# First mixer's input projection: a pipeline in program order with sums held in PSUM, and a last group that alternates convolution and attention blocks

## The chip, the cores and the metric

The kernel runs on one core of one Trainium2 chip. The metric is device time in microseconds (us) of one execution. TensorE (PE) multiplies matrices into PSUM, VectorE (DVE) and ScalarE (ACT) work on tiles elementwise, GpSimd (POOL) builds masks, and SyncE (SP) issues the DMAs that bring data from device memory. PEld is the weight load of TensorE, which overlaps with its matmuls.

## What is computed

Two layers on one sequence of 256 positions with 2048 features, all in float32. Each layer normalises x, scales and shifts it by a modulation (a matrix-vector product with the activated vector `c`), mixes along the sequence, and adds an MLP. The change touches the modulation, the norm and the mixer of layer 0, cut here to its frame:

```python
c_act = jax.nn.silu(c)
mod = jnp.einsum('bd,de->be', c_act, mod_w[layer]) + mod_b[layer]
sh1, sc1, g1, sh2, sc2, g2 = [m[:, None, :] for m in jnp.split(mod, 6, axis=-1)]
h = rms_norm(x, norm_mix_w[layer]) * (1.0 + sc1) + sh1
proj = jnp.einsum('btd,de->bte', h, w_in)
gq, gk, gv, gz, gb, ga, aq, ak, av = split_sizes(proj, AB_SPLITS)
o_a = gated_deltanet(gq, gk, gv, gz, gb, ga, conv_w, a_log, dt_bias, norm_w)
o_b = chunk_band_attention(aq, ak, av, q_norm_w, k_norm_w, rel_bias)
mix = jnp.einsum('bte,ed->btd', jnp.concatenate([o_a, o_b], axis=-1), w_out)
x = x + g1 * mix
```

`gated_deltanet` runs a causal convolution of width 4 over its q, k and v, normalises q and k, and solves a triangular system for each chunk of positions; `chunk_band_attention` normalises q and k and attends over the sequence with a bias. Each has eight heads of width 128, worked on in two groups of four.

## The kernel before

Activations lie with features on partitions. A **unit** is a block of 512 normalised features: four tiles of 128 features by 256 positions. The input projection is cut into **items**: one item multiplies one unit (a "row group" `kg`, 0 to 3) by one block of 512 output columns, with one 1 MB weight block (`w[kg, c0]`, a tile of 128 x 2048, two halves of 1024). The blocks are named by their columns: `GQ`, `GK`, `GV` for the delta net's q, k, v (two blocks each, the second `GQ + 1` and so on), `AQ`, `AK`, `AV` for attention, `GZ` for the gate. A convolution-type item (`b_item`, line 501) has the weights as the stationary operand and matmuls 256 wide; an attention-type item (`a_item`, line 527) has the activations stationary and matmuls 512 wide.

A product in float32 is made in one of two ways. **Split**: weights and activations are each cut into a high part of reduced precision and a remainder. ACT casts the weights to `wh` (line 317), DVE subtracts to get `wl` (line 321), and PE adds three products, `wh` by high, `wh` by remainder, `wl` by high. **Whole**: one plain float32 matmul (two records in the trace) on the loaded weights, with neither cast nor subtraction; it needs an unsplit copy of the unit, `hw`. Before, only the last unit has `hw` (`norm_unit` with `whole`, line 849).

The modulation is 192 sums on DVE (line 439, `mod_job`): each takes a 1 MB matrix `mraw` (128 x 2048), multiplies it by the row vector `crow` and adds along the row, which gives one column of 128 values. Additions of the bias and the scale's gain (lines 447 and 449) finish two columns at a time. The unit of row group `kg` needs shift (`v` = 0) and scale (`v` = 1) for four columns.

The program is written out as one stream. `emit` loads and splits an item's weights one item ahead of its matmuls. After each piece of an item `tick` advances a list of short tasks (`fast`: evacuations, norms), a list of background work (`bg`: the chunk solve, the attention scores) and, by `rate`, the generator of modulation sums. A scheduler then fixes the order on each engine; instructions passed to `keep_in_program_order` stay where they are written. SP's queue issues the loads in order, each waiting for its buffer: four `raw` buffers for weights and modulation matrices together, four pairs of `wh` and `wl`, 18 unit buffers `u`.

In `run` (line 1536) the start loads x, takes square sums (ten narrow matmuls with `ones`, lines 809 to 834) and makes eight modulation sums for unit 0 before the first weights. Row groups 0 to 2 (the **head**) then run the same eight items, `GK, GQ, GV, GK + 1, GQ + 1, GV + 1, AQ, AK`. The first two keep their sums over the groups in PSUM buffers `pm`; the other six go through `pg`, of which there are two: each item's result is copied (line 1590) or added on DVE (line 1592) to a partial sum in a unit buffer. The last group runs the eight items with row group 3, with the remaining attention and gate blocks (all four row groups each) between them, while the chunk solve runs in the background: transposes of `gX`, products `gX` by `gLt`, a masked copy `gY` (DVE, line 1108), products `gXt` by `gY`, and a subtraction from `gX` (DVE, line 1114). Then the output projection starts (`pw`).

## Time and profile before

| | us |
|---|---|
| runs of the kernel before | 2718.03 (median), 2714.11, 2718.79 |
| the profiled execution, own time | 2719.37 |
| its span, first to last instruction | 2717.6 |
| mean granted TensorE clock | 0.998 |
| first weight matmul starts | 40.16 |
| row groups 0 to 2 end | 185.79 |
| output projection starts | 491.30 |

The page gives each engine's busy time and share of the span; the windows view the same for stretches of it. The chain that ended last is followed back from the last instruction, each step to what released it. A timeline row has start, length, engine, line, operation, output<-input, shapes and count; in brackets the idle time before it and the releaser. Groups of instructions have a count, then busy time and mean ns of one.

### The profile page before, as it was taken

To read this page: it belongs to the slowest core of one execution; us is meant where nothing else is said; L and a number is where in the kernel's file an instruction comes from. 1 tells how busy PE (TensorE), PEld (TensorE's weight loads), DVE (VectorE), ACT (ScalarE), POOL (GpSimd) and SP (SyncE) were. 2 spreads that over 40 slices of the span, in tenths; PEclk is the share of its full clock that TensorE was granted. 3 is DMA by queue.
4 is the path that set the end of the run, shared out by engine and by line. 5 is a ranking of instruction groups with operands and counts; after the bars stand their busy time and mean duration, and the time that the engine had idled before them with its cause. 6 is when DMAs were issued, how large, how long until landed. Compare 5 with 4: busy or idle time off the path is not lost.

```text
span 2717.6 us, 39677 instructions
## 1 busy us (share of the span) xinstructions
PE 2665.0 (98%) x15664; PEld 2350.4 (86%) x15664; DVE 2147.6 (79%) x3081; ACT 1351.2 (50%) x1976; POOL 24.5 (1%) x98
## 2 busy tenths in 40 slices
PE   5999999999999999999999999999999999999999
PEld 5887989888888888888888888888888888888888
DVE  7998998987888888889889876897777855555554
ACT  3444454546445354454556544665555354454452
POOL 1000000000000000000000000000000000000000
PEclk9999999999999999999999999999999999999999
DMA  9986487867899898988456665554558855555554
GB/s 341 353 325 235 172 301 272 294 241 282 322 339 328 328 336 330 333 331 307 165 185 217 217 234 200 203 185 172 196 177 293 324 201 188 188 191 193 186 192 134
DMA packets 100459, 680.06 MB, mean 250 GB/s; under 512 B 11185, under 2 KB 14513, under 8 KB 19377
## 3 DMA queue, kind: packets, MB, share of 16 engines
q1 hardware_dynamic: 95376, 669.07, 68.5%
q10 hardware_dynamic: 4896, 8.46, 1.0%
q8 instruction: 123, 2.02, 0.3%
q14 instruction: 64, 0.52, 0.1%
HBM read 675.33 MB, written 2.16 MB: 249 GB/s over the span
## 4 chain that ended last, share of the span: by engine, by line
PE 90%; DVE 6%; DMA 1%; ACT 1%; issue 1%; SPq 0%; ACTq 0%; DVEq 0%
PE pw L308 70%; PE pg L308 13%; PE pm L311 4%; PE pm L308 3%; DVE mraw L439 2%; DVE wl L321 1%; PE pm L314 1%; DMA mraw<-in_mod_dram 1%; DVE u L1592 0%; ACT wh L317 0%; DVE hf L862 0%; ACT pm L1042 0%; DMA raw<-in_w_ab_dram 0%; DMA x<-in_x_dram 0%; DVE u L865 0%
## 5 line engine op out<-in xcount | busy, mean ns | idle before, releaser
L317 ACT CAST wh<-raw 128x1024 fp32r<-128x1024 f32 x870 | 907.1, 1051 | 1031.6 <-PE pw L308 732.9
L321 DVE TENSOR_TENSOR wl<-raw,wh 128x1024 fp32r<-128x1024 f32 x870 | 1048.7, 1220 | 463.8 <-ACT wh L317 349.6
L308 PE MATMUL pw<-u,wh 128*128 128x512 f32 x5584 | 1321.6, 391 | 2.6 <-DVE pad L973 1.9
L308 PEld LDWEIGHTS pw<-u,wh 128*128 128x128 f32 x5584 | 1032.2, 188 | 208.2 <-issue 3.3
L308 PEld LDWEIGHTS pw<-u,wl 128*128 128x128 f32 x5584 | 702.3, 191 | 21.3 <-issue 2.1
L308 PE MATMUL pw<-u,wl 128*128 128x256 f32 x5584 | 714.5, 283 | 0.3 <-DVE wl L321 0.3
L439 DVE SCALAR_TENSOR_TENSOR mraw<-mraw,crow 128x2048 f32<-128x2048 f32 x192 | 438.0, 2283 | 17.8 <-DMA mraw<-in_mod_dram 17.5
L308 PE MATMUL pg<-wh,u 128*128 128x512 f32 x864 | 281.6, 397 | 0.0
L308 PEld LDWEIGHTS pg<-wh,u 128*128 128x128 f32 x864 | 161.9, 188 | 32.1 <-issue 0.5
L925 DVE SCALAR_TENSOR_TENSOR x<-pw,mod,x 128x256 f32<-128x256 f32 x352 | 161.1, 478 | 22.6 <-PE pw L308 20.3
L308 PE MATMUL pg<-wl,u 128*128 128x512 f32 x432 | 169.9, 393 | 0.7 <-DVE wl L321 0.5
L308 PE MATMUL pg<-u,wh 128*128 128x256 f32 x672 | 124.6, 285 | 0.0
L308 PEld LDWEIGHTS pg<-u,wh 128*128 128x128 f32 x672 | 105.7, 192 | 0.3
L308 PEld LDWEIGHTS pg<-wl,u 128*128 128x128 f32 x432 | 81.4, 188 | 17.6 <-DVE wl L321 2.1
L308 PE MATMUL pg<-u,wl 128*128 128x256 f32 x336 | 95.3, 284 | 0.0
L308 PE MATMUL pm<-u,wh 128*128 128x256 f32 (+1 forms) x304 | 64.6, 310 | 19.2 <-ACT wh L317 19.2
L308 PEld LDWEIGHTS pm<-u,wh 128*128 128x128 f32 x304 | 49.1, 198 | 20.3 <-ACT wh L317 20.0
L308 PEld LDWEIGHTS pg<-u,wl 128*128 128x128 f32 x336 | 64.4, 192 | 0.1
L984 DVE SCALAR_TENSOR_TENSOR u<-pad,cst,u 128x256 f32<-128x256 f32 x144 | 60.6, 477 | 3.3 <-ACT u L978 3.2
L864 ACT ACTIVATE u<-hf,mod 128x256 fp32r<-128x256 f32 x64 | 29.3, 502 | 53.0 <-DVE hf L862 53.0
L1504 ACT ACTIVATE rl<-rs 128x512 f32<-128x512 f32 x64 | 40.4, 632 | 18.9 <-DVE rs L1499 14.4
L308 PE MATMUL pm<-u,wl 128*128 128x256 f32 x176 | 46.1, 290 | 3.1 <-DVE wl L321 3.1
(299 smaller groups left out, 1580.5 us busy)
## 6 DMA issues: line engine op xcount, KB each, us to landing
raw<-in_w_dram SPq DMA_DIRECT2D x256, 1024.0 KB, 5.0
mraw<-in_mod_dram SPq DMA_DIRECT2D x192, 1024.0 KB, 6.0
raw<-in_w_ab_dram SPq DMA_DIRECT2D x56, 1024.0 KB, 5.7
raw<-in_w_ssd_dram SPq DMA_DIRECT2D x48, 1024.0 KB, 4.9
raw<-in_w_sz_dram SPq DMA_DIRECT2D x32, 1024.0 KB, 4.9
raw<-in_wo_ssd_dram SPq DMA_DIRECT2D x32, 1024.0 KB, 4.8
raw<-in_wo_ab_dram SPq DMA_DIRECT2D x16, 1024.0 KB, 5.2
sE<-sd_rowd ACTq DMA_DIRECT2D x32, 256.0 KB, 4.9
```

The costliest lines, as they stand in the source:

```text
L308: self.nc.tensor.matmul(o, a, b, start=start, stop=stop, skip_group_check=True)
L311: self.nc.tensor.matmul(o, lhsT, rhs, start=True, stop=True, skip_group_check=True)
L314: self.nc.tensor.transpose(o, a, self.ident[:k, :k])
L317: a = self.nc.scalar.copy(hi, src)
L321: b = self.nc.vector.tensor_tensor(lo, src, hi.bitcast(F32), op=ALU.subtract)
L439: x = nc.vector.scalar_tensor_tensor(raw, raw, 1.0, self.crow, op0=ALU.mult, op1=ALU.mult, accum_out=t[:, f : f + 1])
L864: nc.scalar.activation(hi, h[:, f], AF.Identity, bias=shift[:, col])
L925: nc.vector.scalar_tensor_tensor(x[:, 2 * b + f], ps[:, f, n], g[:, 2 * cb + f : 2 * cb + f + 1], x[:, 2 * b + f], op0=ALU.mult, op1=ALU.add)
L984: nc.vector.scalar_tensor_tensor(h, pad[:, f, 1 + q : 257 + q], w[:, q, j : j + 1], h, op0=ALU.mult, op1=ALU.add)
L1504: nc.scalar.activation(rl, lo, AF.Relu)
```

## The change

**Start.** The loads stand in the order that the code gives. Square sums are accumulated on DVE (seven additions 512 wide) and need four narrow matmuls. One scale column is computed on PE: its matrix is packed as `mod0` for the stationary side, and 16 plain float32 matmuls one column wide give it (`mod_pe`). The norm's transposes stand behind them. `norm_first` multiplies x by the row factors `R` (DVE), scales and shifts on ACT, and keeps the unsplit unit for every row group. The first half unit needs two modulation columns only.

**Head.** `in_order` keeps all its instructions in program order, and `in_units` loads weights as two 512 KB halves into unit buffers (19 now), so that `raw` buffers hold modulation matrices only. Four first halves come first (`k0` whole, `q0` split, `v0` whole, `k1` split), then the second halves and the rest of row group 0, then groups 1 and 2. An item's matmuls over two or three row groups follow each other where listed, with the sum kept in PSUM and evacuated once, by ACT copies. The 24 items are 14 of convolution and 10 of attention type (18 and 6 before); three attention items, one convolution item and two convolution halves are whole (none before). Modulation sums have fixed places: 32 stand ahead of the head's end (31 before).

**Last group.** 18 convolution and 14 attention items (14 and 18 before), six and one of them whole (three and two before), alternating, with the last additions made in the conversion (`att_v`, `conv` write into the partial tile). `rate` goes from 0 to 0.25, 0.6, 1.1 and 0.5. `conv`'s second part has a priority of 100.

```diff
-        self.u_p = pool("up", 18)
+        self.u_p = pool("up", 19)
...
+    def mod_pe(self, raw, o):
+        for k in range(16):
+            self.mmx(o, raw[:, k * P : k * P + P], self.cact[:, k : k + 1], k == 0, k == 15)
...
+            if units:
+                raw = [self.unit(shape=[P, 1024]) for _ in hfs]
+                for hf, r in zip(hfs, raw):
+                    self.dma(r, src[:, 1024 * hf : 1024 * hf + 1024])
...
+    def norm_first(self, cb, key, acts, now=False):
...
+        for b in range(2):
+            self.ordered(nc.vector.tensor_tensor(x[b], self.x[cb][:, 2 * b : 2 * b + 2], self.row(self.R, 2), op=ALU.mult))
+            if now and b == 0:
+                yield
+        yield
+        for b in range(2):
+            for f in range(2):
+                col = slice(cb * 4 + 2 * b + f, cb * 4 + 2 * b + f + 1)
+                self.ordered(nc.scalar.activation(x[b][:, f], x[b][:, f], AF.Identity, scale=scale[:, col], bias=shift[:, col]))
+            self.split(x[b], p[b][:, :, 0], p[b][:, :, 1])
...
+        chunk("k0", 0, True, (0,))
+        raws = [self.mod_load(mod[0, 0, 2])]
+        chunk("q0", 0, False, (0,))
+        raws.append(self.mod_load(mod[0, 1, 2]))
+        self.mod_sum(raws[0], 0, 0, 2)
+        chunk("v0", 0, True, (0,))
+        raws += [self.mod_load(mod[0, v, 3]) for v in range(2)]
+        self.mod_sum(raws[1], 0, 1, 2)
+        for v in range(2):
+            self.mod_fin(0, v, slice(2, 3))
+        chunk("k1", 0, False, (0,))
+        for v in range(2):
+            self.mod_sum(raws[2 + v], 0, v, 3)
+        for v in range(2):
+            self.mod_fin(0, v, slice(3, 4))
+        unit0.finish()
+        self.constants2()
+        self.tail = lambda: None
+        group(0, [("v0", 0, False), ("k1", 0, False), ("k0", 0, True), ("q0", 0, True),
+                  ("q1", 0, False), ("v1", 0, False), ("aq", 0, True), ("ak", 0, True)], (4, 6))
+        group(1, [("aq", 1, False), ("ak", 1, False), ("k0", 1, True), ("q0", 1, True),
+                  ("av", 0, True), ("av", 1, True), ("aq1", 0, True), ("aq1", 1, True)], (0,))
+        group(2, [("av", 2, False), ("aq1", 2, False), ("k0", 2, True), ("q0", 2, True),
+                  ("v0", 1, True), ("v0", 2, True), ("k1", 1, True), ("k1", 2, True)], (0,))
...
-        partial_item(3, 0)
-        partial_item(3, 1)
-        self.a_block(w, AV, get, lambda ps: put("v0", self.att_v(ps)))
-        partial_item(3, 2)
...
+        chunk("k0", 3, True)
+        self.tail()
+        self.in_order = False
+        chunk("v0", 3, True)
+        for kg in (2, 3):
+            chunk("aq", kg, kg == 3)
+        chunk("k1", 3, True)
+        for kg in (2, 3):
+            chunk("ak", kg)
+        chunk("q0", 3, True)
         self.n_item(i["w_gb"], get, 16, self.gdn_gates)
...
+        chunk("av", 3)
+        chunk("q1", 1)
+        gdn.append(self.back(self.gdn_group(0, tasks["k0"], tasks["q0"], tasks["v0"], self.res_n)))
```

In `group`, the tuples are block, row group, and whether the sum stays in PSUM; the last argument lists the places of whole items.

SP's queue at the start of the program, behind the loads of x; `mraw` are modulation matrices, `raw` and in the change `u` weights, `cst` the constants. Before:

```order
L436 DMA mraw_14_179<-in_mod_dram 128x2048
L436 DMA mraw_15_182<-in_mod_dram 128x2048
L1557 DMA cst_84<-in_vec_dram 128x835
L436 DMA mraw_16_186<-in_mod_dram 128x2048
L436 DMA mraw_22_208<-in_mod_dram 128x2048
L436 DMA mraw_23_214<-in_mod_dram 128x2048
L436 DMA mraw_24_217<-in_mod_dram 128x2048
L436 DMA mraw_25_220<-in_mod_dram 128x2048
L436 DMA mraw_26_223<-in_mod_dram 128x2048
L482 DMA raw_27_229<-in_w_ab_dram 128x2048
```

The change, from the packed column `mod0` on:

```order
L454 DMA mraw_6_141<-in_mod0_dram 128x2048
L454 DMA mraw_7_143<-in_mod_dram 128x2048
L454 DMA cst_84<-in_vec_dram 128x835
L454 DMA mraw_8_146<-in_mod_dram 128x2048
L454 DMA u_28_221<-in_w_ab_dram 128x1024
L454 DMA mraw_29_274<-in_mod_dram 128x2048
L454 DMA u_30_276<-in_w_ab_dram 128x1024
L454 DMA mraw_35_292<-in_mod_dram 128x2048
L454 DMA u_36_295<-in_w_ab_dram 128x1024
L454 DMA mraw_39_323<-in_mod_dram 128x2048
L454 DMA mraw_40_325<-in_mod_dram 128x2048
L454 DMA u_41_331<-in_w_ab_dram 128x1024
```

The first weights stand behind four modulation matrices and not eight, as half a block, and half blocks and matrices take turns.

DVE's queue where the weights of the first items are split (`wl`). Before, with the rest of unit 0 (`u_33`) between:

```order
L321 TENSOR_TENSOR wl_29_232<-raw_27_229,wh_28_231 128x1024
L321 TENSOR_TENSOR wl_31_236<-raw_27_229,wh_30_235 128x1024
L376 TENSOR_SCALAR cst_84<-cst_84 128x8
L376 TENSOR_SCALAR cst_84<-cst_84 128x64
L865 SCALAR_TENSOR_TENSOR u_33_290<-hf_35_298,mod00_123,u_33_290 128x256
L321 TENSOR_TENSOR wl_38_308<-raw_36_305,wh_37_307 128x1024
L321 TENSOR_TENSOR wl_40_312<-raw_36_305,wh_39_311 128x1024
L439 SCALAR_TENSOR_TENSOR mraw_43_341,mod00_123<-mraw_43_341,crow_98 128x2048
L321 TENSOR_TENSOR wl_46_371<-raw_44_368,wh_45_370 128x1024
L321 TENSOR_TENSOR wl_48_375<-raw_44_368,wh_47_374 128x1024
```

In the change, `wl_43` is the fourth half's remainder, `u_25` the remainder of unit 0's second half, and `wl_47` the remainder of the fifth half, `v0`'s second; left out are five constants:

```order
L323 TENSOR_TENSOR wl_43_334<-u_41_331,wh_42_333 128x1024
L435 SCALAR_TENSOR_TENSOR mraw_39_323,mod00_123<-mraw_39_323,crow_98 128x2048
L435 SCALAR_TENSOR_TENSOR mraw_40_325,mod01_124<-mraw_40_325,crow_98 128x2048
L448 TENSOR_TENSOR mod00_123<-mod00_123,cst_84 128x1
L448 TENSOR_TENSOR mod01_124<-mod01_124,cst_84 128x1
L450 SCALAR_TENSOR_TENSOR mod01_124<-mod01_124,cst_84 128x1
L323 TENSOR_TENSOR u_25_217<-hw_27_219,u_25_217 128x2x256
...
L378 TENSOR_SCALAR cst_84<-cst_84 128x64
L323 TENSOR_TENSOR wl_47_367<-u_45_364,wh_46_366 128x1024
L323 TENSOR_TENSOR wl_52_400<-u_50_397,wh_51_399 128x1024
```

Two sums, the finishing operations and the constants now stand between the fourth half's remainder and the fifth's, where one sum stood between four remainders.

PE's queue in the last group, in the second group's chunk solve; `pg` rows are an item's large matmuls, all others background (`aq` rows are transposes of the attention query). Before:

```order
L308 MATMUL pg_615_3811<-wh_657_4033,u_211_1715 128x512
L311 MATMUL pm_578_3630<-gY_574_3611,gXt_555_3530 128x128 x4
L311 MATMUL pm_579_3636<-gY_576_3619,gXt_558_3543 128x128 x4
L314 MATMUL pm_580_3650<-ident_86,gX_570_3590 128x128 x4
L311 MATMUL pm_581_3656<-gX_570_3590,gLt_554_3525 128x128 x4
L308 MATMUL pg_615_3811<-wl_658_4034,u_211_1715 128x512
L314 MATMUL pm_583_3664<-ident_86,gX_572_3597 128x128 x4
L311 MATMUL pm_584_3670<-gX_572_3597,gLt_557_3538 128x128 x4
L308 MATMUL pg_615_3811<-wh_657_4033,u_211_1715 128x512 x2
L308 MATMUL pg_615_3811<-wl_658_4034,u_211_1715 128x512
L308 MATMUL pg_615_3811<-wh_657_4033,u_211_1715 128x512 x2
L311 MATMUL pm_592_3696<-gY_582_3661,gXt_555_3530 128x128 x4
```

The change:

```order
L309 MATMUL pg_658_3918<-u_24_216,wh_637_3831 128x256 x2
L309 MATMUL pg_658_3918<-u_24_216,wl_638_3832 128x256
L312 MATMUL pm_582_3543<-gY_578_3520,gXt_548_3380 128x128 x4
L315 MATMUL pm_586_3573<-ident_86,gX_555_3417 128x128 x4
L312 MATMUL pm_587_3579<-gX_555_3417,gLt_544_3362 128x128 x4
L315 MATMUL pm_589_3587<-ident_86,gX_557_3424 128x128 x4
L312 MATMUL pm_590_3593<-gX_557_3424,gLt_547_3375 128x128 x4
L315 MATMUL pm_599_3621<-ident_86,aq_572_3489 128x128 x4
L312 MATMUL pm_600_3627<-gY_588_3584,gXt_545_3367 128x128 x4
L312 MATMUL pm_601_3633<-gY_591_3598,gXt_548_3380 128x128 x4
L315 MATMUL pm_603_3647<-ident_86,gX_555_3417 128x128 x4
L312 MATMUL pm_604_3653<-gX_555_3417,gLt_544_3362 128x128 x4
```

Large and small matmuls took turns every few rows; now a run of 28 such rows of four, 112 matmuls in all, stands with no large one between, of which the first ten are shown.

More of the change, by code (lines that the diff above doesn't have):

```diff
@@ L936, in conv @@
         nc = self.nc
-        dst = self.unit()
+        dst = self.unit() if part is None else part
         for b in range(2):
@@ L1576, in run @@
+        banks, parts = {}, {}
+        tasks = {n: Slot() for n in kinds}
         self.fast_n, self.bg_n = 2, 0.0
@@ new lines, in chunk, with group, load, sums @@
+            if not keep:
+                del banks[n]
+            end = kg == 3 or not keep
+            if kind:
+                self.a_item(psum, w[kg, c0], lambda: unit_now(kg), first, end, after, whole)
+            else:
+                self.b_item(psum, w[kg, c0], lambda: unit_now(kg), first, end, after, whole, hfs)
+        def group(kg, seq, whole):
+            unit = Task(self.norm_first(kg + 1, mix0, acts))
+            vf = [(v, f) for f in range(4 * kg + 4, 4 * kg + 8) for v in range(2)]
+            loads = []
+            def load(n):
+                while len(loads) < min(n, 8):
+                    v, f = vf[len(loads)]
+                    loads.append(self.mod_load(mod[0, v, f]))
+            done = 0
+            def sums(due):
+                nonlocal done
+                while done < due:
+                    v, f = vf[done]
+                    self.mod_sum(loads[done], 0, v, f)
+                    done += 1
+                    if v:
+                        self.mod_fin(0, 0, slice(f, f + 1))
+                        self.mod_fin(0, 1, slice(f, f + 1))
+                    if done == 4:
+                        unit.step()
+            for n, (name, k, keep) in enumerate(seq):
+                chunk(name, k, n in whole, (1,) if kg == 0 and n < 4 else (0, 1), keep)
+                if n == 0:
+                    self.tail()
+                due = n if kg else (0, 1, 1, 2, 4, 5, 7, 7)[n]
+                load(due + 2 if kg else (1, 1, 2, 4, 5, 7, 7, 8)[n])
+                if n == 3:
+                    unit.step()
+                sums(due)
+            def tail():
+                sums(8)
+                unit.finish()
+            self.tail = tail
```

244 lines of the change are left out of this document (139 added, 105 removed).

## The prediction

> **What bounds the kernel now.** I read the page first: busy time by engine, then the chain that ended last.
>
> ```profile
> PE 2665.0 (98%) x15664; PEld 2350.4 (86%) x15664; DVE 2147.6 (79%) x3081; ACT 1351.2 (50%) x1976; POOL 24.5 (1%) x98
> PE 90%; DVE 6%; DMA 1%; ACT 1%; issue 1%; SPq 0%; ACTq 0%; DVEq 0%
> ```
>
> PE is busy nearly throughout, so time can go only where PE waits, or where its own work grows or shrinks. The windows view, cut where the change cuts, shows where the waiting is (length, then busy time of PE, weight loads, DVE, ACT, POOL; granted clock, DMA share, GB/s):
>
> ```profile
> 0.00:40.00 40.00, 8.71 (x38) 7.91 (x38) 29.04 (x59) 10.60 (x21) 8.33 (x38) 1.00 0.93 351
> 40.16:185.79 145.63, 141.09 (x1008) 133.01 (x1009) 133.83 (x161) 60.70 (x76) 0.00 (x0) 1.00 0.94 346
> 185.79:491.30 305.51, 300.26 (x1967) 265.52 (x1966) 274.42 (x573) 156.28 (x396) 13.91 (x38) 0.99 0.69 246
> 491.30:2717.60 2226.30, 2214.93 (x12654) 1943.97 (x12653) 1710.29 (x2291) 1123.40 (x1483) 2.27 (x22) 1.00 0.68 243
> ```
>
> Four stretches: the start, the first three row groups ("head"), the last group with token mixing, and the rest, which the change leaves alone. The start has 31 us of idle PE; the head only 4.5 and the last group 5.3. The head is nearly full on three sides: PE 141, DVE 134 of 146 us, DMA share 0.94. The chain in order of time (start, length, what) tells what fills the start:
>
> ```profile
> 2.17 6.27 DMA x<-in_x_dram
> ...
> 11.01 4.41 PE pm L308 x20
> ...
> 15.92 2.30 DVE mraw L439 x2
> ...
> 30.89 4.43 DVE mraw L439 x4
> ...
> 40.16 1.22 PE pm L308 x4
> ```
>
> After x lands (8.44) and the square sums, the chain is eight modulation sums on DVE, one after the other, until 37.7. The first weight matmul cannot start before all eight.
>
> **The change, part by part.** *Start.* The DMA view of the first 60 us gives GB/s in slices of 1.5 us; the waits view says what SP's queue waited for (total, times, longest); a row of PE's timeline gives the narrow matmul (start, length), and three rows of the head's costliest groups (busy time and mean ns of one behind the bar) give the small pieces: a 512-wide addition, a finishing operation, ACT's scale and shift.
>
> ```profile
> GB/s 0 179 376 396 421 437 431 431 401 441 431 421 175 240 415 311 421 300 421 404 311 273 382 284 426 355 371 344 284 229 431 306 415 328 371 317 333 246 426 350
> SPq L436 <- DVE rsy L276: 12.8, 1, 12.8
> SPq L482 <- DVE wl L321: 47.9, 17, 5.4
> 11.85 3.55 PE L308 MATMUL pm<-ones,sq 128*128 128x1 f32 x16
> L1592 DVE TENSOR_TENSOR u<-pg,u 128x512 f32<-128x512 f32 x22 | 14.3, 682 | 0.9 <-PE pg L308 0.9
> L447 DVE TENSOR_TENSOR mod<-mod,cst 128x2 f32<-128x2 f32 x12 | 1.9, 158 | 0.3
> L864 ACT ACTIVATE u<-hf,mod 128x256 fp32r<-128x256 f32 x11 | 5.5, 509 | 13.8 <-DVE hf L862 13.8
> ```
>
> While its queue is full, the DMA moves about 431 GB/s, so a 1 MB load (1.05e6 bytes) lands every 2.4 us. The changed SP queue holds x, one sum's matrix (10.9), the packed column for PE (13.3), a matrix (15.7), the constants (16.8), a matrix (19.2), then half a weight block (20.4). The packed column takes 16 matmuls; eight of them (two records each) took 3.55 us, so 0.44 each: 13.3 to 20.4. The norm's transposes stand behind them on PE (21.1), the copy of R after them (21.5). DVE's third sum ends at 19.2 + 2.2 = 21.4, the 512-wide product (0.68, as the addition) at 22.2, six finishing operations of 0.16 at 23.2, ACT's scale and shift (0.51) at about **23.8**. Against 40.16 that is **-16.3**. One of the 192 sums and six of the ten matmuls for the square sums go too, but they end before 13.3 and gain nothing more.
>
> *Cold PE and the first four halves.*
>
> ```profile
> 45.21 0.57 PE L308 MATMUL pm<-u,wh 128*128 128x256 f32 x2
> 45.62 0.28 PE L308 MATMUL pm<-u,wl 128*128 128x256 f32 x1
> 45.74 0.40 PE L308 MATMUL pm<-u,wh 128*128 128x256 f32 x2
> ...
> 48.60 0.40 PE L308 MATMUL pm<-u,wh 128*128 128x256 f32 x2
> 184.66 0.39 PE L308 MATMUL pg<-wl,u 128*128 128x512 f32 x1
> ...
> 185.56 0.39 PE L308 MATMUL pg<-wh,u 128*128 128x512 f32 x1
> 185.79 0.63 PE L308 MATMUL pm<-u,wh 128*128 128x256 f32 x4
> 229.75 7.03 PE L308 MATMUL pg<-raw,hw 128*128 128x512 f32 x16
> 236.71 0.30 PE L314 MATMUL pm<-ident,nb 32*128 32x32 f32 x2
> 245.88 4.05 PE L308 MATMUL pg<-hw,raw 128*128 128x256 f32 x18
> 249.77 0.49 PE L314 MATMUL pm<-ident,aq 128*128 128x128 f32 x3
> ```
>
> From 45.74 to 48.60 stand 24 split matmuls: a warm half of a convolution item takes 2.88, the item 5.76. The first half took 40.16 to 45.74 = 5.58, so a cold start costs 2.7. A split attention item is 24 matmuls at 0.226 (five from 184.66 to 185.79): 5.44. An item on unsplit ("whole") weights took 229.75 to 236.71 for attention; for convolution 18 records took 3.89, so 32 take 6.9. I use 6.9 for both: whole costs PE +1.16 (convolution) or +1.46 (attention).
>
> The four halves, whole and split in turn, end at 23.8 + 12.7 + 2.7 = 39.2. There PE waits, because the fifth half needs unit 0's second half, with modulation columns 2 and 3. The fourth half's weights land after three more half blocks and four matrices (20.4 + 3 x 1.2 + 4 x 2.4 = 33.6); its cast (1.05) and remainder (1.22) end at 36.0. Behind that remainder DVE's queue holds two sums (2.2 each, 40.4) and three finishing operations (40.9); ACT scales and copies (0.5 + 0.6, 42.0); DVE makes the unit's remainder (0.7, 42.8), seven constants (about 0.17 each, as the finishing operation, 44.0), and only then the fifth half's weight remainder: **45.2**. A wait of **6.0** that the trace of before does not show. Bounds: 2 (loads and casts come early, so that DVE has done the sums while PE works) and 9 (every load at 351 GB/s, 0.6 later for each MB). I take 6, as it follows step by step from rows.
>
> ```profile
> 427.94 1.09 PE L314 MATMUL pm<-ident,aq 128*128 128x128 f32 x4 [2.02 <-DVE aq L1250]
> 428.00:432.00 4.00, 4.00 (x23) 4.00 (x24) 2.76 (x4) 1.65 (x3) 0.00 (x0) 0.59 0.81 309
> ```
>
> After 2.02 us of idle PE the granted clock was 0.59 for 4 us, which loses 1.6. The wait of 6 will cost that at least, and up to the 2.7 of a cold start: I put **2**. The Trainium skill ("TensorE: Matmul & The Clock Gate", on the efficiency rules at its end) warns of idle gaps over about 3 us between bursts of matmuls; this trace lost the clock after 2.0, so a shorter wait is not free either. By the page alone the short-wait rival below would keep its clock and be 1.6 faster still.
>
> *Rest of the head.* The 24 items become 14 convolution and 10 attention, 135.0 as split, plus whole: four halves' worth of convolution (2.3) and three attention items (4.4) = 141.7, against 18 x 5.76 + 6 x 5.44 = 136.3. Less the first four halves 12.7, 129.0 remain: head ends at 45.2 + 2 + 129.0 = **176.2**, against 185.8: **-9.6**, if nothing else waits. DVE decides that:
>
> ```profile
> L321 DVE TENSOR_TENSOR wl<-raw,wh 128x1024 fp32r<-128x1024 f32 x48 | 56.7, 1219 | 9.9 <-ACT wh L317 9.5 <-issue 0.3
> L439 DVE SCALAR_TENSOR_TENSOR mraw<-mraw,crow 128x2048 f32<-128x2048 f32 x24 | 54.8, 2282 | 0.2 <-DMA mraw<-in_mod_dram 0.2
> L1590 ACT COPY u<-pg 128x512 f32<-128x512 f32 x12 | 6.4, 587 | 15.7 <-PE pg L308 15.7
> ```
>
> Sums held in PSUM take 22 additions off DVE (14.3), whole items ten remainders (12), as five items' worth go in unsplit. DVE is then behind PE at the wait only, ahead of it after about 65 us. Evacuations are ACT copies, and ACT has over half its time free. DMA must bring 32 sums' matrices, 24 items and x: 58 MB x 2.4 = 140 us of 176. Without that margin the head waits for loads (a rival).
>
> *Last group.* Its mix of 14 convolution and 18 attention items becomes 18 and 14 (+1.3), six convolution and one attention item whole instead of three and two (+2.0): **+3.3**. Its waits I leave at the 5.3 of before: the longest shown, on the query normalisation, moves with its items, and a second evacuation from PSUM before the second item (1 us) may replace it.
>
> *Sum.* -9.6 + 3.3 = **-6.3**: own time of the profiled execution 2719.4 (span 2717.6 and 1.8 around it) gives 2713.1; from the median 2718.0, 2711.7. I write **2712**.
>
> The Trainium skill ("FP8 and Floating Point Precision", TensorE Precision Notes) counts four passes for true FP32, one more than the three split products; by 4/3 the whole items would cost 4.5 more than my rows give. Here two records of a whole item took 1.20 times the split's three products, and I go by that.
>
> **Rivals.**
>
> *Mixing stands alone (slower).* The change groups the last group's items so that the chunk solve's small matmuls run in rows of 112, 50, 48, 38 and 34 with nothing large between. Before they were mostly in pieces of 4 to 30, and one run of 50:
>
> ```profile
> 282.00:292.00 10.00, 10.00 (x86) 9.72 (x85) 9.92 (x24) 5.85 (x15) 1.12 (x4) 1.00 0.39 123
> 284.45 0.42 DVE L1108 TENSOR_TENSOR gY<-pm,lev 128x256 f32<-128x256 f32 x1
> 287.31 0.41 DVE L1114 TENSOR_TENSOR gX<-gX,pm 128x256 f32<-128x256 f32 x1
> 289.28 0.60 PE L314 MATMUL pm<-ident,gX 128*128 128x128 f32 x4
> 289.72 1.06 PE L311 MATMUL pm<-gX,gLt 128*128 128x128 f32 x8
> ```
>
> A round of one chain is transposes 0.44, product 0.9, DVE 0.42, product 0.9, DVE 0.41 and some 0.4 of signalling: 3.5 us, during which the two chains give PE 4.5. So it is covered by 1 us, and is not once a 1.2 us weight remainder or 2.28 us sum stands ahead on DVE. At 1 us in each of 12 rounds: +12, **2724**. For it: DVE is 90% busy here. Against: the run shown had DVE at 99% and no idle PE. Deciding point: more than 1 us of foreign DVE work per round.
>
> *Loads bound the head (same).* At the 346 GB/s that the head shows, 61e6 bytes take 177 us from the first, so the head ends about 181: **2717**. For: DMA share 0.94 already. Against: slices at 431, and SP's waits there are for buffers (47.9 us for weight buffers in the first 160 us), which the change adds to by keeping weights elsewhere.
>
> *The wait is short and idle goes (faster).* If DVE has done its sums while PE works, the wait is 2 and the clock costs 1.6: 4.4 less; with half of the last group's idle time gone, 2.6 more: **2705**. For it: DVE is idle in the start for longer than now. Against: the two matrices land only at 30 and 32.4.
>
> *The start hardly moves.* If the packed column's matmuls, with a weight load of 128 columns each, take twice the 0.44 of the row, the head starts at 31 and not at 24, and what the change is said to bring is gone: 2712 + 7 = **2719**. Against: the row's matmuls have the same shape.
>
> **How the numbers follow.** Chances: forecast (2708 to 2716) 0.45, short wait 0.18, loads 0.17, start 0.07, mixing alone 0.13. The range reaches from the short-wait case, with 2 below it, to the mixing case: 2703 to 2724, which leaves out some 0.15. 0.2%, about what a measurement of this kernel can tell from no change, is 5.4 us: faster begins below 2712.6, slower above 2723.5. Some 0.27 of the forecast's chance lies below 2712.6, and the short wait's 0.18: faster 0.45. Slower is the mixing case, 0.13. The rest is the same, 0.42.
>
> **What would show it.** The first weight matmul (now on an unsplit half) near 23.8; a wait before the fifth half of about 6 us with the wl of line 323 as releaser, and a clock below 1 behind it; the first three groups' end near 176; the output projection's start about 6 us before 491.3; idle PE during the run of 112 under 2 us. Wrong if PE waits for loads in the head (DMA as releaser), or if the background waits for gY or gX in the last group.

## The result

The change made the kernel **slower by 0.78%**: median 2738.0 us of four runs (2736.0 to 2738.6) against 2716.6 of four (2714.1 to 2718.8), ratio 1.0078 with a 95% interval of 1.0060 to 1.0095. The prediction said 2712, with 2703 to 2724 as its range. The profiled execution took 2737.9, its span 2736.2. Its page, engines and chain that ended last:

```profile
PE 2687.4 (98%) x15588; PEld 2360.4 (86%) x15588; DVE 2120.5 (77%) x3049; ACT 1344.1 (49%) x1964; POOL 24.8 (1%) x98
PE 90%; DVE 5%; DMA 3%; ACT 1%; issue 1%; SPq 0%; DVEq 0%; ACTq 0%
```

PE is as full as before, with 22 us more of it, although it has fewer instructions. The windows of the changed kernel, cut at the same places as before, show where (columns as in the prediction):

```profile
0.00:40.00 40.00, 27.48 (x125) 24.78 (x126) 25.79 (x46) 12.49 (x21) 8.34 (x38) 0.97 0.97 391
23.20:177.47 154.27, 148.44 (x857) 127.02 (x857) 122.41 (x159) 62.33 (x81) 0.00 (x0) 0.97 0.95 369
177.47:502.55 325.08, 309.14 (x2033) 276.33 (x2031) 265.03 (x564) 151.58 (x387) 14.13 (x38) 0.98 0.61 218
502.55:2736.20 2233.65, 2216.89 (x12646) 1944.94 (x12644) 1717.52 (x2294) 1121.27 (x1481) 2.28 (x22) 1.00 0.68 243
```

Stage by stage; the output projection's row ends at the same matmul in each kernel (644.4 before, 663.4 in the change):

| us | before | forecast | change |
|---|---|---|---|
| first weight matmul | 40.2 | 23.8 | 23.2 |
| head, from there | 145.6 | 152.4 | 154.3 |
| last group | 305.5 | 308.8 | 325.1 |
| output projection and early MLP | 153.1 | 153.1 | 160.9 |
| rest | 2073.3 | 2073.3 | 2072.8 |

Each stage is read from one execution; the one of the kernel before took 2719.4, 2.8 us above that kernel's median. Up to the head's end the forecast holds within 1.3 us (177.5 against 176.2). Two losses stand behind it: 16 us in the last group and 8 in the output projection.

The start went as worked out, and the wait before the fifth half came in two pieces. Chain of the change in order of time, then PE's timeline:

```profile
5.13 14.03 DMA mraw<-in_mod_dram
...
19.18 2.30 DVE mraw L435 x2
21.48 0.66 DVE hw L895
...
22.36 13.20 DMA u<-in_w_ab_dram
...
37.89 4.42 DVE mraw L435 x4
...
46.57 7.79 PE pg L309 x46
```

```profile
23.16 5.75 PE L309 MATMUL pm<-hw,u 128*128 128x256 f32 x16 [2.15 <-ACT hw L902]
...
36.68 0.50 PE L309 MATMUL pg<-u,wh 128*128 128x256 f32 x2 [1.44 <-ACT wh L319]
37.94 0.58 PE L309 MATMUL pg<-u,wl 128*128 128x256 f32 x1 [0.76 <-DVE wl L323]
38.32 0.63 PE L309 MATMUL pg<-u,wh 128*128 128x256 f32 x2
...
38.96 0.63 PE L309 MATMUL pg<-u,wh 128*128 128x256 f32 x2
...
45.23 0.80 PE L309 MATMUL pg<-u,wh 128*128 128x256 f32 x2 [3.08 <-ACT wh L319]
46.57 0.58 PE L309 MATMUL pg<-u,wl 128*128 128x256 f32 x1 [0.55 <-DVE wl L323]
```

The sum at 19.18 still waits for its matrix. The fourth half's weights land at 35.6 (forecast 33.6), so PE waits 1.4 us ahead of that half and 0.8 inside it. The two sums at 37.89 stand ahead of the fifth half, which begins at 45.23 and, with its first remainder made, runs from 46.57 (forecast 45.2).

**First loss.** The chunk solve of the second group of heads starts with a preparation, in which PE and other engines hand small tiles to each other: products with `gu`, a reciprocal root, `gV`, `gXt`, until the first product with `gX` can run. PE's timeline there, and the window behind the first wait:

```profile
393.75 0.39 PE L309 MATMUL pg<-wh,u 128*128 128x512 f32 x1
399.52 2.05 PE L312 MATMUL pm<-u,u 128*128 128x128 f32 x8 [5.39 <-DVE gV L1125]
404.21 1.12 PE L315 MATMUL pm<-ident,gXt 128*128 128x128 f32 x4 [2.63 <-DVE gXt L1138]
406.91 1.11 PE L315 MATMUL pm<-ident,gXt 128*128 128x128 f32 x4 [1.59 <-DVE gXt L1138]
399.50:412.00 12.50, 8.26 (x36) 7.58 (x37) 10.98 (x20) 4.31 (x15) 0.53 (x1) 0.50 0.67 232
```

PE finishes its last attention item at 394 and then waits 5.4, 2.6 and 1.6 us for DVE, at half clock between. DVE's queue at that place:

```profile
388.43 0.68 DVE L1125 TENSOR_TENSOR gV<-pm,gnk 128x512 f32<-128x512 f32 x1
...
390.39 2.28 DVE L435 SCALAR_TENSOR_TENSOR mraw<-mraw,crow 128x2048 f32<-128x2048 f32 x1
...
394.33 2.28 DVE L435 SCALAR_TENSOR_TENSOR mraw<-mraw,crow 128x2048 f32<-128x2048 f32 x1
...
396.69 1.22 DVE L323 TENSOR_TENSOR wl<-raw,wh 128x1024 fp32r<-128x1024 f32 x1
...
398.69 0.69 DVE L1125 TENSOR_TENSOR gV<-pm,gnk 128x512 f32<-128x512 f32 x1
```

Between the first and the second `gV` stand two modulation sums, three weight remainders (two left out) and the steps of a reciprocal root.

**Second loss.** PE, ACT and SP in the output projection:

```profile
581.89 0.51 PE L309 MATMUL pm<-ones,ss 128*128 128x1 f32 x4
585.51 0.97 PE L309 MATMUL pw<-u,wh 128*128 128x512 f32 x3 [3.11 <-ACT wh L319]
588.22 1.01 PE L309 MATMUL pm<-ones,sq 128*128 128x1 f32 x4 [1.74 <-ACT sq L855]
584.41 2.00 ACT L319 CAST wh<-raw 128x1024 fp32r<-128x1024 f32 x2 [9.39 <-DMA raw<-in_wo_ab_dram]
565.33 10.51 SPq L454 DMA_DIRECT2D mraw<-in_mod_dram  x4
578.06 2.88 SPq L454 DMA_DIRECT2D raw<-in_wo_ab_dram  x2
```

The last weights of the output projection are issued late, behind a run of modulation matrices; ACT is idle 9.4 us until they land. In SP's queue four matrices stand together ahead of them: 64 sums were asked for before the projection (67 before the change), and the norm behind it needs 80.

### The profile page after: what moved, and what is told of

Read it like the earlier page. It is cut to its first block, busy times and chain, and to the rows that moved or that the text cites. A ratio compares the mean times of both kernels' runs of the same rounds, so it can differ in the third digit from the quotient of the medians.

```text
span 2736.2 us, 39518 instructions
## 1 busy us (share of the span) xinstructions
PE 2687.4 (98%) x15588; PEld 2360.4 (86%) x15588; DVE 2120.5 (77%) x3049; ACT 1344.1 (49%) x1964; POOL 24.8 (1%) x98
## 4 chain that ended last, share of the span: by engine, by line
PE 90%; DVE 5%; DMA 3%; ACT 1%; issue 1%; SPq 0%; DVEq 0%; ACTq 0%
PE pw L309 69%; PE pg L309 14%; PE pm L312 4%; PE pm L309 2%; DMA mraw<-in_mod_dram 2%; DVE mraw L435 2%; PE pm L315 1%; DVE wl L323 1%; DMA u<-in_w_ab_dram 0%; ACT wh L319 0%; DMA raw<-in_w_ab_dram 0%; DVE x L980 0%; DMA sE<-sd_rowd 0%; ACT pm L1098 0%; DVE u L1015 0%
## 5 line engine op out<-in xcount | busy, mean ns | idle before, releaser
L319 ACT CAST wh<-raw 128x1024 fp32r<-128x1024 f32 x818 | 854.6, 1051 | 1010.9 <-PE pw L309 707.2
L323 DVE TENSOR_TENSOR wl<-raw,wh 128x1024 fp32r<-128x1024 f32 x818 | 987.3, 1220 | 449.1 <-ACT wh L319 339.6
L309 PE MATMUL pg<-wh,u 128*128 128x512 f32 x832 | 272.5, 398 | 0.0
L980 DVE SCALAR_TENSOR_TENSOR x<-pw,mod,x 128x256 f32<-128x256 f32 x352 | 160.9, 478 | 16.3 <-PE pw L309 14.1
L309 PE MATMUL pg<-u,wh 128*128 128x256 f32 x592 | 114.1, 292 | 4.5 <-ACT wh L319 4.5
L309 PEld LDWEIGHTS pg<-u,wh 128*128 128x128 f32 x592 | 95.8, 197 | 5.7 <-ACT wh L319 5.1
L309 PEld LDWEIGHTS pg<-wl,u 128*128 128x128 f32 x416 | 78.3, 188 | 15.9 <-issue 1.2
L309 PE MATMUL pg<-u,wl 128*128 128x256 f32 x296 | 86.5, 292 | 1.3 <-DVE wl L323 1.3
L319 ACT CAST wh<-u 128x1024 fp32r<-128x1024 f32 x38 | 39.3, 1048 | 44.6 <-DMA u<-in_w_ab_dram 22.4
L323 DVE TENSOR_TENSOR wl<-u,wh 128x1024 fp32r<-128x1024 f32 x38 | 45.6, 1222 | 19.7 <-ACT wh L319 19.5
L1564 ACT ACTIVATE rl<-rs 128x512 f32<-128x512 f32 x64 | 40.4, 631 | 17.1 <-DVE rs L1559 12.5
L309 PE MATMUL pm<-u,wh 128*128 128x256 f32 (+1 forms) x224 | 48.0, 310 | 0.0
L1559 DVE TENSOR_TENSOR rs<-pw,rs 128x512 f32<-128x512 f32 x64 | 43.7, 683 | 5.2 <-ACT rs L1558 5.2
```

The costliest lines, as they stand in the source:

```text
L309: self.nc.tensor.matmul(o, a, b, start=start, stop=stop, skip_group_check=True)
L319: a = self.nc.scalar.copy(hi, src)
L323: b = self.nc.vector.tensor_tensor(lo, src, hi.bitcast(F32), op=ALU.subtract)
L980: nc.vector.scalar_tensor_tensor(x[:, 2 * b + f], ps[:, f, n], g[:, 2 * cb + f : 2 * cb + f + 1], x[:, 2 * b + f], op0=ALU.mult, op1=ALU.add)
L1559: nc.vector.tensor_tensor(lo, ps[:, :, 0], lo, op=ALU.add)
L1564: nc.scalar.activation(rl, lo, AF.Relu)
```

## The experiments

Each run changes the changed kernel unless it says otherwise; "last group" is the head's end to the output projection, measured as in the table.

**The rates of the modulation sums.** `x1_gate_rate` asks for four more sums during the gate items:

```diff
-        self.rate = 0.5
+        self.rate = 0.7
         self.b_block(w, GZ, get, ...)
...
+        self.rate = 0.5
         self.out_blocks(i["wo_ab"], ...)
```

> The changed kernel with four more modulation sums in the two gate items of the last group (rate 0.7 there, 0.5 again from the output projection on); nothing else. Theory 'modulation timing': the 8 us that the output projection lost (waits of 3.1 and 1.7 us and the low clock behind them) go, since no four matrices stand ahead of its last weights; the 16 us at the second group's chunk solve (394 to 412 us) stay: about 2730. Rival 'item order': the loss in the output projection comes from how late the last items end, not from the matrices: 2737 to 2738.

Measured 2733.9, ratio 1.0064 (1.0049 to 1.0079). The output projection, in the change and here:

```profile
502.55:663.40 160.85, 153.71 (x874) 133.79 (x873) 144.36 (x211) 81.68 (x113) 0.00 (x0) 0.98 0.76 279
```

```profile
505.60:658.10 152.50, 150.89 (x873) 131.78 (x873) 134.88 (x201) 81.22 (x113) 0.00 (x0) 1.00 0.75 274
```

8 us go there once the four matrices are asked for earlier, so they are the second loss. The last group grew from 325.1 to 328.9 with the four sums, which gives back half.

`x2_rates_before` sets 0.25 for 0 and 0.6; `x3_quiet_solve` puts the sums early and late, away from the second solve (rates 0.6, 0.3, 0.2, 0.1, 1.15):

> The changed kernel with the modulation rates of the kernel before in the last group (0.25 up to the second chunk solve, where the change has 0, 0.25 and 0.6; then 1.1 and 0.5 in both). Theory 'modulation timing': 67 sums stand ahead of the output projection as before, so its 8 us go, and part of the 16 us at the second chunk solve, where fewer matrices are queued: 2722 to 2730. Rival 'item order': the waits at the second chunk solve stay in full, as PE's queue has no large matmul left there: 2730.

> The changed kernel with the modulation sums moved off the second chunk solve: rate 0.6 in the first part of the last group, 0.3, 0.2 and 0.1 around the second solve, 1.15 in the gate items, 0.5 from the output projection on. Theory 'modulation timing': both losses go, 8 us and most of 16: 2714 to 2720. Rival 'item order': only the 8 us go, and PE still waits 5 us or more for gV before the second solve: 2728 to 2731.

Measured 2736.7 (1.0064 to 1.0094) and 2743.5 (1.0088 to 1.0122), last groups 330.1 and 330.4. In x3 the wait for `gV` fell from 5.4 to 0.3 us, but waits of 3 to 5 us came at 196, 246, 256 and 507 us. Both expectations failed, and other rates only move the waits: in x2 the wait for `gV` stayed, at 5.9 us, and 5.0 us of waits came ahead of it, at 193 to 247. What x3 shows of the preparation itself comes below.

`x4_no_priority` (`priority(0)` for `priority(100)` in `conv`):

> The changed kernel without the priority of 100 in the second part of the convolution (0 in its place). Theory 'modulation timing': the priority has no part in either loss: 2735 to 2740. Rival 'item order': a convolution that is put off makes the second chunk solve late, so without the priority the wait for gV shrinks by several us: 2730 or less.

Measured 2739.2 (1.0073 to 1.0103): the priority has no part.

**Sums, or the order of the items?** `y1_short_sums` cuts each sum from the head's end to the output projection's last block to 64 of 2048 columns (`self.cols`) and leaves the rest of the sum out; the loads stay:

```diff
+        n = self.cols
...
-            x = self.nc.vector.scalar_tensor_tensor(raw, raw, 1.0, self.crow, ...)
+            x = self.nc.vector.scalar_tensor_tensor(raw[:, :n], raw[:, :n], 1.0, self.crow[:, :n], ...)
```

> The changed kernel with the modulation sums between the head's end and the output projection's last block cut to 64 of 2048 columns (so their values are left incomplete); their loads stay as they are. Theory 'sums on DVE': the 2.28 us sums stand ahead of the second chunk solve's chain on DVE; without them the waits for gV and gXt go and the last group takes 308 to 313 us instead of 325, while the output projection keeps most of its 8 us, since its last weights still land behind four matrices: 2722 to 2727. Rival 'item order': the waits come from where the solve stands on PE, and the last group stays above 320: 2733 or more. Rival 'loads': DMA is what is late, nothing changes: 2738.

Measured 2718.6 (1.0000 to 1.0020), the last group:

```profile
177.60:486.30 308.70, 303.89 (x2033) 272.31 (x2032) 203.84 (x565) 151.24 (x388) 14.48 (x38) 1.00 0.63 229
```

308.7 is the forecast's 308.8, with 4.8 us of idle PE. So without the sums' time on DVE the 16 us go, and the loads, which stayed, are not their cause. The output projection kept only half of its loss, at 156.6 us, where most of it was expected to stay. But the kernel before carries as many sums with 5.3 us idle. `y3_old_item_order` puts the changed kernel's items in the order of before:

```diff
         chunk("k0", 3, True)
-        chunk("v0", 3, True)
-        ...
+        chunk("q0", 3, True)
+        chunk("av", 3)
+        chunk("v0", 3, True)
+        self.n_item(i["w_gb"], get, 16, self.gdn_gates)
+        for kg in (2, 3): chunk("aq", kg, kg == 3)
+        for kg in (2, 3): chunk("ak", kg)
+        gdn.append(...)
...
```

> The changed kernel (start, head, sums in PSUM, whole items, 64 KB less nothing else changed) with the last group's items in the order of the kernel before: k0, q0, av, v0, gates, aq, ak, first chunk solve, k1, attention, q1, v1, aq1, second solve, and the rates of before (0.25, then 1.1, 0.5). Theory 'item order': the last group takes 308 to 311 us and the output projection 153, so the start's gain shows: 2714 to 2719. Rival 'sums on DVE', with the same sums in the same number before the output projection: the waits at the second solve stay in large part: 2726 to 2733.

(The words on 64 KB in it are a slip and mean nothing.) Measured 2729.2 (1.0038 to 1.0068), last group 321.0. Neither theory: the waits for `gV` are gone, but 7.9 us of waits stand at 203 to 217, behind the convolutions of three items on DVE with sums between them, and 4.8 more at 367 to 371, for the cast and the remainder of an item's weights.

`z2_sums_late` is x1 with the sums put off on DVE:

```diff
-        with self.priority(20):
+        with self.priority(20 if self.in_order else 300):
             x = self.nc.vector.scalar_tensor_tensor(raw, raw, 1.0, self.crow, ...)
```

> The changed kernel with the gate items' rate of the run x1 (0.7) and modulation sums put off behind other DVE work in the last group (priority 300 in place of 20), their loads and number unchanged. Theory 'sums on DVE': where a sum stands in DVE's queue decides; idle PE in the last group falls from 18 to under 12 us: 2722 to 2729 against 2734 of x1. Rival 'composition': DVE's whole load against the cover is what counts, the waits only change place: 2731 to 2737.

Measured 2720.5 (1.0006 to 1.0024), last group 311.6 with 8.1 us idle. The number of sums is the same, so their place matters. With that and the constants moved, `b1_both_mended` gave 2719.4 (1.0005 to 1.0022), above the 2717 expected at most. With even rates `b2_mended_even` gave 2724.8 (1.0021 to 1.0045): 5 us of waits came at 193 to 247, so early sums cost again:

> The changed kernel with both losses mended: gate items' rate 0.7 (0.5 again at the output projection), modulation sums put off in the last group alone (priority 300 there, 20 elsewhere), and the constants behind row group 0. Theory 'sums on DVE': head to 177, last group 309 to 312, output projection 153: own time of the profile 2712 to 2717, level with the kernel before or up to 4 us faster. Rival 'composition': a last group above 315 and 2719 or more.

> As b1, with the sums spread more evenly over the last group (rates 0.25, 0.4, 0.5, 0.7, 0.85 in place of 0, 0.25, 0.6, 1.1, 0.7). Theory 'sums on DVE': fewer matrices meet the second chunk solve, idle PE falls further, 2 us or so below b1. Rival 'composition': the early sums meet the convolutions instead and it is no better than b1, or 2 to 4 us worse.

`c1_before_sums_late` puts the sums off in the kernel **before**:

> The kernel before, with nothing changed but the modulation sums of its last group put off behind other DVE work (priority 300 in place of 20). Theory 'items make the sums' place matter': its last group has only 5 us of idle PE and gains 0 to 2 us: 2713 to 2717 beside 2715 to 2716. Rival 'sums always cost': it gains like the changed kernel, 5 us or more: 2710 or less.

Measured 2717.3 (0.9996 to 1.0015): no gain. The sums' place matters only with the changed items.

**The head, and the old items.** `h1_constants_late` moves `constants2()` behind row group 0; `h2_head_split` splits four whole items (`()` for the places of whole items):

> The changed kernel with the preparation of the constants (seven short DVE operations and two on ACT) moved behind row group 0, out of the wait before the fifth half. By the prediction's chain (wait ends with the remainder of the fifth half's weights on DVE, with the constants ahead of it) the fifth half starts about 1 us earlier and the head ends 1 us earlier; the rest unchanged: 2736 to 2738. If loads end that wait, nothing moves.

> The changed kernel with the four whole items of the head's row groups (one convolution, three attention items) split instead; the two whole first halves stay. By the prediction's prices PE saves 1.2 + 3 x 1.5 = 5.5 us and DVE gets 9.8 us more to do, of which it has about 25 us free between 40 and 180: the head ends 4 to 5.5 us earlier and the total falls as much, 2732 to 2734. If loads bound the head (DMA share 0.95 to 0.98 there), it ends at the same time: 2737 to 2739.

h1: 2735.0 (1.0062 to 1.0092), fifth half 0.3 us earlier, not 1. h2: 2735.3 (1.0051 to 1.0085); the head took 154.1, as before the edit: PE's busy time fell by 2.3, and new waits of 1.8 and 0.8 at 68 us took their place. There ACT's casts stand behind a scaling that waits 6.5 us for DVE's modulation columns; in the change it waits 4.2 us, while PE works on a whole item, which needs no cast. So the whole items cost PE time and cover a wait for DVE, and taking them away gains the head nothing.

`s1_old_items` keeps the new start and head, with the items of before:

```diff
+        for kg in (1, 2):
+            group(kg, [("k0", kg, True), ("q0", kg, True), ("v0", kg, False), ("k1", kg, False),
+                       ("q1", kg, False), ("v1", kg, False), ("aq", kg, False), ("ak", kg, False)], ())
...
+        self.a_block(w, AV, get, lambda ps: put("v0", self.att_v(ps)))
```

> The new start and the head in program order with weights in unit buffers, but the items of the kernel before: eight items in each of row groups 0 to 2 (partial sums added on DVE again), the blocks av and aq1 whole in the last group, its order, its whole items and its rates as before. Theory 'composition' (the change took attention items, which ask little of DVE, out of the last group and left convolution items in it, so DVE's sums of 2.28 us meet the convolutions and the solve without cover): the last group takes 305 to 309 us as before and the output projection 153, and the start's gain shows in part: 2702 to 2712. Rival 'start' (what the earlier start gains, DVE and DMA take back somewhere before the output projection, whatever the items): the last group or the head grows and the total is 2715 or more.

Measured 2717.3 (0.9998 to 1.0017). Head and last group:

```profile
23.70:186.10 162.40, 147.78 (x993) 137.55 (x994) 142.54 (x185) 67.72 (x84) 0.00 (x0) 0.96 0.90 342
186.10:492.10 306.00, 301.09 (x1967) 265.03 (x1966) 274.37 (x573) 155.61 (x393) 14.09 (x38) 0.99 0.68 246
```

The last group is back at 306, but the head takes 162, and the start's 16 us are gone: idle PE in the head is 14.6 us against 5.8 in the change. The largest waits are 4.4 us ahead of the fifth half, 2.1 at 68 us as in h2, and 2.5 at 169 us for a partial sum that is added on DVE again.

**Where the solves stand.** What remained was why the changed items make the sums hurt. `d1_solve_later` starts the second solve behind the block `ak1`:

> The run x1 (changed kernel, gate items' rate 0.7) with one line moved: the second chunk solve is started behind the four items of the block ak1, not ahead of them, so that five items and not one stand between v1's last item and it, as before the change. Theory 'cover': the waits for gV and gXt at the solve's start (11 us in x1) fall to under 2 and the last group from 329 to 312 to 317 us: 2717 to 2723. Against it: the solve's end moves towards the gate items that need it and PE waits there instead, or the sums meet the solve as before: the last group stays above 323 and 2729 or more.

Measured 2739.3 (1.0072 to 1.0106). One wait of 7.9 us for `gV` stays. The last group is shorter, 318 us, but only because the attention waits later: the output projection takes 164 us, with waits of 3.4 and 1.7 at 508 to 513. A later solve gains nothing, which left the opposite to try: the solves are too late. PE's rows for the gates, the second solve's first product `gu`, the first `gX` product and the last attention-type matmul, before, in the change (its last attention row, 393.75, is above) and in d2:

```profile
241.91 0.36 PE L311 MATMUL pm<-gd_g,Umask 128*128 128x8 f32 x2 [0.41 <-DVE gd_g L1007]
365.07 1.88 PE L311 MATMUL pm<-gu,SUmask 128*128 128x512 f32 x4
391.00 1.06 PE L311 MATMUL pm<-gX,gLt 128*128 128x128 f32 x8
415.32 0.39 PE L308 MATMUL pg<-wh,u 128*128 128x512 f32 x1
```

```profile
254.94 0.36 PE L312 MATMUL pm<-gd_g,Umask 128*128 128x8 f32 x2
380.31 1.12 PE L312 MATMUL pm<-gu,SUmask 128*128 128x512 f32 x2 [0.55 <-ACT gu L1102]
407.82 3.62 PE L312 MATMUL pm<-gX,gLt 128*128 128x128 f32 x16
```

```profile
239.93 0.36 PE L312 MATMUL pm<-gd_g,Umask 128*128 128x8 f32 x2
360.67 1.88 PE L312 MATMUL pm<-gu,SUmask 128*128 128x512 f32 x4
385.91 2.00 PE L312 MATMUL pm<-gX,gLt 128*128 128x128 f32 x16
419.92 0.39 PE L309 MATMUL pg<-wh,u 128*128 128x512 f32 x1
```

The preparation from `gu` to `gX` takes 26 to 28 us in the first two, with some 10 us of sums on DVE beside it in each. Before, attention items run until 24 us behind its end; in the change they end 14 us ahead of it. The gates stand 56 us from the head's end before and 77 in the change. `d2_solves_earlier` is x1 with this order:

```diff
+        chunk("q0", 3, True)
+        self.n_item(i["w_gb"], get, 16, self.gdn_gates)
         chunk("k1", 3, True)
         for kg in (2, 3):
             chunk("ak", kg)
-        chunk("q0", 3, True)
-        self.n_item(i["w_gb"], get, 16, self.gdn_gates)
+        gdn.append(self.back(self.gdn_group(0, ...)))
         chunk("av", 3)
         chunk("q1", 1)
-        gdn.append(self.back(self.gdn_group(0, ...)))
```

> The run x1 (changed kernel, gate items' rate 0.7) with q0 and the gates moved ahead of k1 and ak, and the first solve started two items earlier, ahead of av and q1's first; nothing else. Theory 'solves too late': gates and both solves come 10 to 17 us earlier, the second preparation (380 to 408 us in x1) finds attention items beside it, its waits (11 us) go, and the last group falls from 329 to 311 to 317: 2717 to 2722. Rival 'crowded convolutions': three convolutions at the front keep DVE full, PE waits there instead as in the run with the old order, and the last group stays above 319: 2725 or more.

Measured **2716.7** (0.9991 to 1.0011), against 2733.9 of x1. Its last group:

```profile
177.66:487.30 309.64, 304.48 (x2024) 271.94 (x2023) 269.52 (x570) 150.22 (x385) 14.36 (x38) 1.00 0.65 236
```

The preparation is still 25 us long, with 6.9 us of sums beside it, but attention items run until 34 us behind its end, and the waits are gone. The run x3 shows the other way out. Its gates come later still, at 275.9, but no sum stands beside the preparation:

```profile
377.41 1.12 PE L312 MATMUL pm<-gu,SUmask 128*128 128x512 f32 x2 [0.55 <-ACT gu L1102]
...
383.36 2.05 PE L312 MATMUL pm<-u,u 128*128 128x128 f32 x16 [0.29 <-DVE gV L1125]
...
393.70 2.00 PE L312 MATMUL pm<-gX,gLt 128*128 128x128 f32 x16
```

It takes 16.3 us there, and as many in y1, and so ends about when the attention items end (393) or before. So the first loss needs both: sums that stretch the preparation from 16 to some 26 us, which the kernel before has too, and attention items that end before it does, which is what the change brought.

d2 has neither loss and is still level with the kernel before, where 6 us less was forecast. Its profile is 3.6 us above the forecast's stages: 1.5 at the head's end, 0.8 in the last group and 1.6 behind the output projection, less 0.3 in it. The other 3 are those by which the profiled execution of the kernel before, from which the stages were forecast, lies above its median. Both are within what one execution differs from the next, and no run splits them further.

**A version that beats both.** `c3_pipeline_old_items` is s1 with what had relieved DVE in the changed head: sums of two row groups held in PSUM, four whole items, and the constants behind row group 0. Its groups, as they differ from the change:

```diff
...
+        group(1, [("aq", 1, False), ("ak", 1, False), ("k0", 1, True), ("q0", 1, True),
+                  ("v0", 1, False), ("k1", 1, False), ("q1", 1, True), ("v1", 1, True)], (0,))
+        group(2, [("q1", 2, False), ("v1", 2, False), ("k0", 2, True), ("q0", 2, True),
+                  ("v0", 2, False), ("k1", 2, False), ("aq", 2, False), ("ak", 2, False)], (0,))
...
```

> The new start and head pipeline with the items of the kernel before (as s1: the blocks av and aq1, the last group's order, whole items and rates as before), but with what relieved DVE in the changed head: sums of two row groups held in PSUM where they follow each other (aq, ak, q1, v1), four whole items, constants behind row group 0. Prices: PE 149 busy in the head, DVE about 128 instead of 142 in s1, so the head takes 155 to 157 instead of 162, the last group 306, the output projection 153: 2709 to 2713, 3 to 6 us faster than before. Rival: loads bound the head (56 MB in it whatever the items), it stays at 160 to 162: 2716.

Measured **2710.6** of eleven runs, ratio to the kernel before 0.9983 (0.9975 to 0.9992). Head and last group:

```profile
23.70:178.60 154.90, 150.13 (x944) 134.41 (x945) 128.99 (x169) 60.27 (x76) 0.00 (x0) 0.97 0.92 358
178.60:485.30 306.70, 301.02 (x1966) 265.23 (x1965) 274.72 (x573) 155.08 (x393) 14.08 (x38) 0.99 0.67 245
```

The head is 7.5 us shorter than in s1 with 13.5 us less work on DVE and the same loads, so loads did not bound it. Which of the three reliefs did it was not tried alone.

## Why the prediction was wrong

- **Start, right.** 23.2 against 23.8; the chain of loads, narrow matmuls and one sum is the one worked out.
- **Four halves, wait, cold clock, right in their sum.** The fifth half runs at 46.6 against 45.2. The waits are 5.8 us against 6.0, but 2.2 of them stand at the fourth half, whose weights landed 2.0 us later than worked out, and 3.6 at the fifth; the four halves ended at 42.1 and not at 39.2.
- **Rest of the head, right in its sum.** It ends at 177.5 against 176.2. That PE bounds it was only half the truth: h2 took work off PE and gained the head nothing, because waits for DVE came in its place.
- **Last group, PE's work, right.** +3.3 was forecast; with the waits taken away (y1, d2) the stage takes 308.7 and 309.6 against 308.8.
- **Last group, waits: the step that failed.** "Its waits I leave at the 5.3 of before" carried the waits over as if they belonged to the items. They belong to the distance between the solves and the large work. The change made `q0` the eighth item where it was the second, with the gates behind it, and took six attention items into the head (four on balance, as two of `aq` and `ak` came back). The chain of solves began later, and the second preparation had nothing beside its last 14 us. Idle PE rose from 5.3 to 15.9, and PE's own time is 5.6 above the forecast's, by the low clock behind the waits: together the 16. A count of the items ahead of the gates, with the prediction's own lengths, shows 39 us before (three convolution items, four attention items) and 51 in the change (five whole, three split): 12 of the 21 us by which the gates moved were there to be read. The gates alone do not make the loss, as x3 shows: it takes a preparation that ends behind the last attention item.
- **Output projection: left out.** The order of SP's queue shows four matrices together ahead of its last weights, and 64 sums ahead of it for 67. The prediction counted sums at the head's end and no further; at 2.4 us a matrix the price was there to be read.
- **The slower rival** (chance 0.13, 2724) had the right sign and stage, and the wrong mechanism: the run of 112 small matmuls itself does not wait.

```profile
412.00:440.00 28.00, 27.81 (x244) 27.64 (x243) 14.05 (x38) 9.36 (x20) 3.99 (x8) 0.98 0.24 86
```

It is what is left when the large work has been used up before the solve. The wait is ahead of it, in the preparation.

Why sums cut short (y1) or put off (z2) help as well follows: both bring the solve forward and shorten its preparation (`gu` at 361 and the first `gX` 16 us behind it in y1, 374 and 22 us in z2). That the earlier order alone suffices, with its sums in place, is shown by d2; what each moved item has of the delay of 21 us was not tried one by one.

## What to carry to other kernels

Before a serial background chain is left "as before", count the large work that stands ahead of its start and beside its longest preparation, in the order of the changed program; work moved out of a stage takes its cover along. Where loads are requested by rate, count the requests at every deadline, not only at the first. An engine's busy share does not show such a loss: DVE is 82% busy in the changed last group, and 90% in that of before, which waits less.

## What the runs showed of the hardware

Short waits cost the clock. In the change 1.44 and 0.76 us of idle PE, with two matmuls between, were followed by 3 us of matmuls at 0.21 us spacing (three from 38.32 to 38.96), where the warm half of the prediction has 0.12; after the 5.4 us wait the granted clock was 0.50 over 12.5 us in which PE was two thirds busy. The Trainium skill ("TensorE: Matmul & The Clock Gate", on the efficiency rules at its end) warns of gaps over about 3 us; in this kernel shorter ones were enough, and the measurement decides.
